# Order of the weight splits and choice of the weight homes in a two-layer decoder trunk

## Chip, cores and metric

One NeuronCore of one Trainium2 chip runs the whole kernel; the other cores are idle. The metric is the device time of one execution in microseconds (us), the median over several executions. PE is the matrix engine (PEld its weight loads), DVE the vector engine, ACT the scalar engine, POOL the general engine that here only issues accumulating transfers, SP the engine that issues the plain transfers.

## What is computed

Two decoder layers on an input of 512 tokens by 1024 features, all in fp32. Each layer is a gated FFN, a mixer and a second gated FFN:

```python
def swiglu(h, w_gate, w_up, w_down):
    return (jax.nn.silu(h @ w_gate) * (h @ w_up)) @ w_down

for l in range(DEPTH):            # 2 layers, D_MODEL 1024, D_FF 2816, SEQ 512
    h = rms_norm(x, gn[0])
    x = x + 0.5 * rms_norm(swiglu(h, ffn1...), gn[1])
    proj = rms_norm(x, gn[2]) @ w_in[l]
    ...
    mixed = jax.nn.sigmoid(gate_a) * y_hg + jax.nn.sigmoid(gate_b) * y_at
    x = x + rms_norm(mixed @ w_out[l], gn[3])
    x = x + 0.5 * rms_norm(swiglu(rms_norm(x, gn[4]), ffn2...), gn[5])
```

`y_hg` is a chunked linear recurrence over four heads, `y_at` a sliding-window attention; the change touches neither. It touches the way the weights of all these products reach PE.

## The kernel before

**Three products for one.** PE multiplies rounded fp32 operands. Every operand is therefore kept as a pair: `hi`, the value rounded by a copy into the matmul type, and `lo`, the remainder. One product is three matmuls, hi·hi, hi·lo and lo·hi (`mm3`). An activation pair is made by `split` (L432 the copy to `hi` on ACT, L433 the subtraction to `lo` on DVE). A weight pair lives in a *home*: two tiles `whi` and `wlo` of 128 x 1024, of which there are six (`WS`).

**The weight stream.** The object `ws` of class `Stream` holds a list of items in the order in which PE uses them. SP loads the raw weights (`w32` in the code, `w` in the profile; L247, 512 KB each) into four slots, in order; a load waits until the last reader of the unit that had the slot is done. `split` (a method of `Stream`, L324 to L373) turns the next item into a home. There are these kinds of items:
- `u`: ACT copies to `whi` (L354), DVE subtracts to `wlo` (L363). The first items of the kernel are of this kind.
- `v`: ACT copies to `whi`, ACT writes minus the weight into `wlo` (L358), and POOL issues a transfer that adds the weight to `wlo` on its way (L361). This takes DVE out of the work.
- `a`, `b`, `c`, `d`: two raw units u and u+1 make one group of a seven-product scheme in the gated FFNs and in the mixers' gates. `a` is unit u, made as `v` is. `b` needs a first sum of the two units (L340, L341 on DVE, into a tile `tt`), then a cast and a DVE subtraction. `c` needs the second sum (L347, L348), then the same. `d`, the half item, is half of unit u+1, 512 columns, made as `v` is; PE uses it four times, the others eight times.
- `p1` to `p7`: quarter items of the FFNs' second product, made by `quarter` (L288 cast, L296 subtraction).

PE uses a, b, c, d of one group in this order, and before the change they are split in this order too. `ahead` keeps some three items split ahead of PE, as homes are free. Before the change the six homes rotate: an item takes the home that is next in turn, and waits until PE has let go of the item that was there.

**Who orders what.** PE's order is the order of the code. The rows of the other engines are put in order by a scheduler, save where the code pins a row to its place in the program (`pin`, and `ws.hold` inside the loop `fast`, where `ws.tight` is set). Each engine then runs its rows strictly one after another: a row that waits for a semaphore holds all rows behind it.

**Stages.** In time: the start (eight column blocks of x are loaded and split, their squares are summed, L462 on ACT and L463 on DVE; `rstd` makes 1/rms, L475 on ACT, L476 and L477 on DVE, and a matmul with `ones` spreads it); then for each layer FFN 1, mixer, FFN 2. An FFN has a loop over groups (`fast`, 84 matmuls of 256 columns a group, DVE steps L1063 to L1087 between the seven products) and a stage `down` of quarter items. There are four such loops: 89 to 233 us (15 groups), 728 to 915, 1062 to 1247 and 1742 to 1928 us (19 groups each). They are called stages 1 to 4 below.

Of the kernel before, what the change touches and what calls it, by code (L numbers as in the profile page):

```python
# [8 lines left out]
F32R = mybir.dt.float32r  # L9
# [6 lines left out]
P = 128  # L16
D = 1024
# [19 lines left out]
W32, WS, AHEAD, TAIL, FIRST, EARLY, LATE = 4, 6, 3, 4, 7, 4, 8  # L37
# [9 lines left out]
def trunk(ctx: ExitStack, tc: tile.TileContext, xin, wall, gains, lbT, hgain, sinks, c_dist, c_mask, c_ident, out):  # L47
    nc = tc.nc
    cp = ctx.enter_context(tc.tile_pool(name="cp", bufs=1))
    sb = ctx.enter_context(tc.tile_pool(name="sb", bufs=1))  # L50
# [9 lines left out]
    def nm(s):  # L60
        seq[0] += 1
        return f"{s}_{seq[0]}"
# [18 lines left out]
    class Order:  # L81
        def __init__(self):
            self.t = 0.0
            self.rest = 0.0
            self.cos = []
# [62 lines left out]
    pin = tc.keep_in_program_order  # L148
# [10 lines left out]
    class Stream:  # L159
        def __init__(self):  # L160
            self.n, self.wall = 0, 0
            self.items = []
            self.raw, self.dma = {}, 0
            self.done, self.flight = 0, 0
            self.cur, self.c = 0, 0
            self.src = {}
            self.pinned = False
            self.most = AHEAD
            self.tight, self.gate = False, None
            self.side, self.freed = [], 0  # L170
            self.part = {}

        def plain(self, n, kind="u", at=0):
# [84 lines left out]
        def quarter(self, it):  # L258

            q, u, v, h = it.q, it.u, it.u + it.n, (slice(0, S), slice(S, D))  # L260

            def sums(o, x, y, op):
                for c in range(2):
                    pin(nc.vector.tensor_tensor(o[c], x[c], y[c], op=op))  # L264

            def raw(i):
                self.load(i + 1)
                return [self.raw[i][:, c] for c in h]

            def leave(i):  # L270
                self.raw.pop(i)
                self.freed += 1
                self.load(self.freed + W32)

            if it.kind in ("p1", "p2"):
                w = raw((u if it.kind == "p1" else v) + q)
            elif it.kind in ("p3", "p5"):
                w = self.b22[q]
            elif it.kind == "p7":

                w = self.b12[q]
                if q == 0:
                    sums(w, w, self.b22[q], ALU.add)
            else:
                w = self.b12[q]
            it.hi, it.lo = (sb.tile([P, D + 64], F32R, tag=t, name=nm(t), bufs=WS)[:, it.at : it.at + D] for t in ("whi", "wlo"))
            for c in range(2):
                i = nc.scalar.copy(it.hi[:, h[c]], w[c])  # L288
                if self.pinned:
                    pin(i)  # L290
            if it.kind == "p7" and q + 1 < it.n:
                sums(self.b12[q + 1], self.b12[q + 1], self.b22[q + 1], ALU.add)
            elif it.kind == "p6":
                sums(self.b22[q], self.b22[q], w, ALU.add)
            for c in range(2):
                pin(nc.vector.tensor_tensor(it.lo[:, h[c]], w[c], it.hi[:, h[c]].bitcast(F32), op=ALU.subtract))  # L296
            if it.kind == "p7":

                sums(w, raw(u + q), w, ALU.subtract)
                leave(u + q)  # L300
            elif it.kind == "p5":
                self.b22[q] = None
                if q + 1 < it.n:
                    sums(self.b12[q], raw(v + q), self.b12[q], ALU.add)
                    leave(v + q)
            elif it.kind == "p4":
                self.b12[q] = None
                if q == 0:
                    i = it.n - 1
                    sums(self.b12[i], raw(v + i), self.b12[i], ALU.add)  # L310
                    leave(v + i)
            self.done += 1
            self.flight += 1
# [5 lines left out]
        def product(self):  # L319
            if self.gate:  # L320
                self.gate()
                self.gate = None

        def split(self):  # L324
            it = self.items[self.done]
            if it.kind[0] == "p":
                return self.quarter(it)
            u, last = it.u, it.kind in "uvd"
            self.load(u + (1 if it.kind in "uv" else 2))
            it.hi, it.lo = (sb.tile([P, D + 64], F32R, tag=t, name=nm(t), bufs=WS)[:, it.at : it.at + D] for t in ("whi", "wlo"))  # L330
            w, h = self.raw[u], (slice(0, D // 2), slice(D // 2, D))
            cols = (slice(0, D),)
            if it.kind == "u" and u < 2:
                cols = h
            if it.kind in "bcd":
                v = self.raw[u + 1]
            if it.kind == "b":

                self.t13 = sb.tile([P, D], F32, tag="tt", name=nm("tt"), bufs=2)
                pin(nc.vector.tensor_tensor(self.t13[:, h[0]], w[:, h[0]], v[:, h[0]], op=ALU.add))  # L340
                pin(nc.vector.tensor_tensor(self.t13[:, h[1]], v[:, h[0]], v[:, h[1]], op=ALU.add))  # L341
                w = self.t13
                self.product()
            elif it.kind == "c":

                t = sb.tile([P, D], F32, tag="tt", name=nm("tt"), bufs=2)
                pin(nc.vector.tensor_tensor(t[:, h[0]], self.t13[:, h[0]], v[:, h[1]], op=ALU.add))  # L347
                pin(nc.vector.tensor_tensor(t[:, h[1]], t[:, h[0]], w[:, h[1]], op=ALU.add))  # L348
                w = t
            elif it.kind == "d":  # L350
                w = v
                cols = h[1:]
            for c in cols:
                i = nc.scalar.copy(it.hi[:, c], w[:, c])  # L354
                if u < 6 or self.pinned or self.tight:
                    pin(i)
                if it.kind in "vad":
                    i = nc.scalar.mul(it.lo[:, c], w[:, c], -1.0)  # L358
                    if self.pinned or self.tight:
                        pin(i)  # L360
                    nc.gpsimd.dma_start(it.lo[:, c].bitcast(F32), w[:, c], accum_op=ALU.add)  # L361
                else:
                    self.hold(nc.vector.tensor_tensor(it.lo[:, c], w[:, c], it.hi[:, c].bitcast(F32), op=ALU.subtract))  # L363
            self.done += 1
            self.flight += 1
            if last:
                nu = u + (1 if it.kind in "uv" else 2)
                for i in range(u, nu):
                    self.raw.pop(i)
                    self.freed += 1  # L370
                self.load(self.freed + W32)

        def ahead(self):  # L373
            while self.done < min(len(self.items), self.cur + 1 + self.most) and self.flight < WS:
                self.split()

        def need(self, i):
            self.ahead()
            while self.done <= i:
                assert self.flight < WS  # L380
                self.split()
            return self.items[i]
# [117 lines left out]
    def pair_split(v, how=split):  # L500
        return how(v, to=(big(F32R, [P, 2, S // 2]), big(F32R, [P, 2, S // 2])))
# [13 lines left out]
    class First(Quarters):  # L515
# [44 lines left out]
        def sums(self):  # L560

            k = len(self.x56)
            a = []
            for i in range(2):
                f = xs[k + 4 * i]
                nc.vector.scalar_tensor_tensor(f, f, g_sb[:, 0, 0, k + 4 * i : k + 4 * i + 1], self.rb, op0=ALU.mult, op1=ALU.mult)
                a.append([f[:, c] for c in HALF])
            self.x124.append([])
            for v in (a[0][0], a[1][0], a[1][1]):
                x = big(F32R, [P, 2, S // 2])  # L570
                split(v, to=(x[:, 0, :], x[:, 1, :]))
                self.x124[k].append(x)
            for x, v in zip((self.x56, self.x37), quarter_sums(a[0][0], a[1][0], a[0][1], a[1][1])):
                x.append(pair_split(v))
# [74 lines left out]
    class Late:  # L649
# [20 lines left out]
        def first(self, k):  # L670
            x = big(F32R, [P, 2, S // 2])
            self.x1.append(split(self.src[k][:, HALF[0]], to=(x[:, 0, :], x[:, 1, :]), hold=pin))
# [979 lines left out]
```

## Time and profile before

| | |
|---|---|
| median of 3 runs | 2052.01 us (2051.7 to 2052.35) |
| profiled execution, its own time | 2052.22 us |
| span of the profile | 2050.4 us |
| granted clock, mean | 0.999 |
| PE busy | 2035.9 us, 99% |
| DVE busy | 1623.6 us, 79% |
| ACT busy | 1250.1 us, 61% |
| POOL busy | 267.6 us, 13% |
| raw weights and other reads | 213.43 MB, 111 GB/s over the span |

Rows of the timeline read: start, duration, engine, line, operation, output tile and input tiles, shape; in brackets how long the engine was idle before the row, and what ended the idle time. A row `x4` is four instructions in succession, and its duration runs from the first start to the last end. A row that begins with two names and an arrow says who waited for what, how long in all, how often, and the longest time. Rows of one engine can overlap by about 0.1 us, since an instruction starts before the one ahead of it has left the pipeline.

### The profile page before, as it was taken

How to read it: one execution, taken by the hardware profiler on the slowest of the kernel's cores; microseconds unless marked ns; L12 is line 12 of the kernel's file. 1: busy time of each engine (PE TensorE's matmuls, PEld its weight loads, DVE VectorE, ACT ScalarE, POOL GpSimd, SP SyncE). 2: the span in 40 equal slices, each digit the busy share in tenths (PEclk: the TensorE clock that was granted, in tenths of full speed). 3: DMA queues.
4: the chain of work that ended last, by engine and by line, in shares of the span. 5: the costliest groups of instructions: out<-in, count | busy, mean ns of one | idle time of the engine just before them, and what ended most of it. 6: DMA issues, size and time to landing. Idle time of an engine off the chain costs nothing. (4 is left out here: it accounts for less than half of the span.)

```text
span 2050.4 us, 36557 instructions
## 1 busy us (share of the span) xinstructions
PE 2035.9 (99%) x13553; PEld 1820.7 (89%) x13553; DVE 1623.6 (79%) x2894; ACT 1250.1 (61%) x2213; POOL 267.6 (13%) x318
## 2 busy tenths in 40 slices
PE   9999999999999999999999999999999999999998
PEld 8899978877888999998899998888778989999977
DVE  5887889767676778888988878987686858788888
ACT  7566687446355556658866566864554545665684
POOL 0111140000000011113201111400000100111140
PEclk9999999999999999999999999999999999999999
DMA  8577798322237367778757878872122563777794
GB/s 257 146 189 193 184 195 238 117 64 71 73 94 215 114 147 190 189 190 205 203 154 188 193 187 205 181 229 92 62 73 62 136 194 102 181 188 190 184 201 123
DMA packets 166802, 328.07 MB, mean 160 GB/s; under 512 B 19072, under 2 KB 85088, under 8 KB 166624
## 3 DMA queue, kind: packets, MB, share of 16 engines
q1 hardware_dynamic: 122416, 228.16, 33.2%
q0 software_dynamic: 44064, 97.54, 28.2%
q8 instruction: 106, 1.74, 0.3%
q14 instruction: 72, 0.59, 0.1%
q10 hardware_dynamic: 144, 0.05, 0.0%
HBM read 213.43 MB, written 14.73 MB: 111 GB/s over the span
## 5 line engine op out<-in xcount | busy, mean ns | idle before, releaser
L116 PE MATMUL acc<-s,whi 128*128 128x256 f32 (+1 forms) x4998 | 1027.5, 305 | 0.0
L116 PEld LDWEIGHTS acc<-s,whi 128*128 128x128 f32 x4998 | 794.7, 188 | 46.5 <-issue 3.2
L116 PE MATMUL acc<-s,wlo 128*128 128x256 f32 (+1 forms) x2488 | 757.0, 304 | 3.3 <-DMA wlo<-w 2.9
L116 PEld LDWEIGHTS acc<-s,wlo 128*128 128x128 f32 x2488 | 469.1, 189 | 28.7 <-DMA wlo<-w 5.0
L116 PE MATMUL acc<-whi,s 128*128 128x512 f32 x1360 | 442.4, 393 | 2.6 <-DVE s L433 1.8
L354 ACT CAST whi<-w 128x1024 fp32r<-128x1024 f32 (+1 forms) x310 | 286.5, 928 | 148.2 <-PE acc L116 105.2
L354 ACT CAST whi<-tt 128x1024 fp32r<-128x1024 f32 x160 | 168.0, 1050 | 250.2 <-DVE tt L348 164.7
L361 POOL DMA_DIRECT2D wlo<-w x178 | 154.0, 867 | 1235.6 <-DVE wlo L363 504.8
L116 PEld LDWEIGHTS acc<-whi,s 128*128 128x128 f32 x1360 | 255.0, 188 | 61.4 <-issue 3.2
L363 DVE TENSOR_TENSOR wlo<-tt,whi 128x1024 fp32r<-128x1024 f32 x160 | 196.0, 1225 | 131.9 <-ACT whi L354 126.0
L116 PE MATMUL acc<-wlo,s 128*128 128x512 f32 x680 | 266.4, 392 | 0.9 <-DVE wlo L296 0.9
L116 PE MATMUL aux<-s,whi 128*128 128x256 f32 (+1 forms) x1296 | 230.0, 280 | 0.0
L363 DVE TENSOR_TENSOR wlo<-w,whi 128x1024 fp32r<-128x1024 f32 (+1 forms) x132 | 157.3, 1205 | 73.9 <-ACT whi L354 73.6
L116 PEld LDWEIGHTS aux<-s,whi 128*128 128x128 f32 x1296 | 197.0, 188 | 1.1 <-issue 0.5
L116 PE MATMUL aux<-s,wlo 128*128 128x256 f32 (+1 forms) x648 | 181.1, 279 | 0.0
L116 PEld LDWEIGHTS acc<-wlo,s 128*128 128x128 f32 x680 | 127.8, 188 | 29.8 <-DVE wlo L296 5.1
L358 ACT ACTIVATE wlo<-w 128x1024 fp32r<-128x1024 f32 (+1 forms) x178 | 153.7, 863 | 0.0
L116 PE MATMUL aux<-whi,s 128*128 128x512 f32 x432 | 144.1, 391 | 0.0
L444 POOL DMA_DIRECT2D s<-s x128 | 111.1, 971 | 216.1 <-ACT s L432 98.1
L116 PEld LDWEIGHTS aux<-s,wlo 128*128 128x128 f32 x648 | 122.1, 188 | 0.5 <-DMA wlo<-w 0.2
L296 DVE TENSOR_TENSOR wlo<-s,whi 128x512 fp32r<-128x512 f32 x160 | 102.7, 685 | 9.9 <-ACT whi L288 6.3
L432 ACT CAST s<-s 128x512 fp32r<-128x512 f32 (+1 forms) x140 | 70.8, 547 | 44.8 <-DVE s L491 39.3
(184 smaller groups left out, 2468.7 us busy)
## 6 DMA issues: line engine op xcount, KB each, us to landing
w<-wall SPq DMA_DIRECT2D x267, 512.0 KB, 4.2
wlo<-w POOLq DMA_DIRECT2D x98, 512.0 KB, 5.2
w<-wall SPq DMA_DIRECT2D x224, 128.0 KB, 3.5
wlo<-w POOLq DMA_DIRECT2D x80, 256.0 KB, 3.3
s<-wall SPq DMA_DIRECT2D x128, 128.0 KB, 4.4
s<-s POOLq DMA_DIRECT2D x64, 256.0 KB, 4.9
x_d<-s SPq DMA_DIRECT2D x48, 256.0 KB, 4.1
s<-x_d SPq DMA_DIRECT2D x48, 256.0 KB, 5.1
```

The source lines that it names most:

```text
L116: nc.tensor.matmul(o, lhsT, rhs, start=start, stop=stop)
L296: pin(nc.vector.tensor_tensor(it.lo[:, h[c]], w[c], it.hi[:, h[c]].bitcast(F32), op=ALU.subtract))
L354: i = nc.scalar.copy(it.hi[:, c], w[:, c])
L358: i = nc.scalar.mul(it.lo[:, c], w[:, c], -1.0)
L361: nc.gpsimd.dma_start(it.lo[:, c].bitcast(F32), w[:, c], accum_op=ALU.add)
L363: self.hold(nc.vector.tensor_tensor(it.lo[:, c], w[:, c], it.hi[:, c].bitcast(F32), op=ALU.subtract))
L432: (hold or ws.hold)(nc.scalar.copy(hi, src))
L444: nc.gpsimd.dma_start(lo.bitcast(F32), src, accum_op=ALU.add)
```

## The change

Three things change in the class `Stream`.
1. **Order of the splits.** A table `plan` puts d ahead of c of the same group: a, b, d, c. Where there is a home left after d, c is split in the same call.
2. **Order inside an item** of the kinds v, a, d: the copy with a minus sign and its transfer come ahead of the cast to `whi`.
3. **Homes.** Each of the six homes is a tile of its own name (`whi0` to `whi5`), and `home` picks the one whose last item was used up longest ago, in place of the rotation.

The raw units are let go after c now, no longer after d, and `need` asks if the item has its home. The diff:

```diff
         self.side, self.freed = [], 0
+            self.own, self.plan = [None] * WS, []
...
-            it.hi, it.lo = (sb.tile([P, D + 64], F32R, tag=t, name=nm(t), bufs=WS)[:, it.at : it.at + D] for t in ("whi", "wlo"))
+            self.home(it)
...
+        def home(self, it):
+
+            k = min((k for k in range(WS) if not self.own[k] or self.own[k].left <= 0), key=lambda k: self.own[k].i if self.own[k] else -1)
+            self.own[k] = it
+            it.hi, it.lo = (sb.tile([P, D + 64], F32R, tag=f"{t}{k}", name=nm(t))[:, it.at : it.at + D] for t in ("whi", "wlo"))
+
         def split(self):
-            it = self.items[self.done]
+            if not self.plan:
+                for i, it in enumerate(self.items):
+                    it.i = i
+                    self.plan.append(i)
+                    if it.kind == "d":
+                        self.plan[-2:] = [i, i - 1]
+            it = self.items[self.plan[self.done]]
...
             for c in cols:
-                i = nc.scalar.copy(it.hi[:, c], w[:, c])
-                if u < 6 or self.pinned or self.tight:
-                    pin(i)
                 if it.kind in "vad":
                     i = nc.scalar.mul(it.lo[:, c], w[:, c], -1.0)
                     if self.pinned or self.tight:
                         pin(i)
                     nc.gpsimd.dma_start(it.lo[:, c].bitcast(F32), w[:, c], accum_op=ALU.add)
-                else:
+                i = nc.scalar.copy(it.hi[:, c], w[:, c])
+                if u < 6 or self.pinned or self.tight:
+                    pin(i)
+                if it.kind not in "vad":
                     self.hold(nc.vector.tensor_tensor(it.lo[:, c], w[:, c], it.hi[:, c].bitcast(F32), op=ALU.subtract))
             self.done += 1
             self.flight += 1
-            if last:
+            if it.kind in "uvc":
...
+            elif it.kind == "d" and self.flight < WS:
+                self.split()
...
-            while self.done <= i:
+            while not hasattr(self.items[i], "hi"):
```

The diff shifts later lines by 14 (L354 becomes L372, L358 becomes L368, L363 becomes L376, L432 becomes L446, L462 becomes L476). PE's order is the same row by row, and so is POOL's; SP's differs in three places by one load that moves ahead of two stores; DVE's differs at the kernel's start and around the mixers' gates. ACT's differs throughout. Three places of it follow; in the names, the number behind `whi`, `wlo`, `s` counts the tiles, and `w_33_174` is the raw unit in a slot.

First ACT at the start of the kernel, with the last four squares of x (`s_203` to `s_212`) and the first weights. Before:

```order
L532 ACTIVATE s_199<-s_77,g_sb 128x512
L462 ACTIVATE s_203<-s_74 128x512
L462 ACTIVATE s_206<-s_75 128x512
L462 ACTIVATE s_209<-s_76 128x512
L462 ACTIVATE s_212<-s_77 128x512
L354 CAST whi_248<-w_18_142 128x1024
L354 CAST whi_278<-w_23_154 128x1024
L354 CAST whi_308<-w_33_174 128x1024
```

and now:

```order
L546 ACTIVATE s_199<-s_77,g_sb 128x512
L372 CAST whi_308<-w_33_174 128x1024
L476 ACTIVATE s_203<-s_74 128x512
L476 ACTIVATE s_206<-s_75 128x512
L476 ACTIVATE s_209<-s_76 128x512
L476 ACTIVATE s_212<-s_77 128x512
L372 CAST whi_248<-w_18_142 128x1024
L372 CAST whi_278<-w_23_154 128x1024
```

The cast of `w_33` moved from behind the four squares and the casts of `w_18` and `w_23` to a place ahead of them all. On DVE its subtraction (`wlo_309`) moved in the same way: it stands ahead of the sums of squares with `s_203`, `s_206` and `s_209` now, and the last sum, with `s_212`, stands behind the subtraction of `w_18` (`wlo_249`).

Second ACT at the start of stage 2, where the last activations of the norm ahead are split (`s` <- `s`, L432). Before:

```order
L1106 ACTIVATE s_7905<-acc_7609 128x512
L432 CAST s_7919<-s_7913 128x512
L432 CAST s_7923<-s_7914 128x512
L354 CAST whi_7928<-tt_7930 128x1024
L354 CAST whi_7935<-w_1389_7568 128x512
L358 ACTIVATE wlo_7936<-w_1389_7568 128x512
L354 CAST whi_7968<-w_1405_7640 128x1024
L358 ACTIVATE wlo_7969<-w_1405_7640 128x1024
L432 CAST s_7983<-s_7977 128x512
```

and now:

```order
L1120 ACTIVATE s_7905<-acc_7609 128x512
L372 CAST whi_7968<-w_1405_7640 128x1024
L446 CAST s_7919<-s_7913 128x512
L368 ACTIVATE wlo_7969<-w_1405_7640 128x1024
L446 CAST s_7923<-s_7914 128x512
L372 CAST whi_7933<-tt_7935 128x1024
L446 CAST s_7983<-s_7977 128x512
```

The cast and the copy of the next group's a (from `w_1405`) moved from behind c's cast to places ahead of and between the casts of the activations; d's pair (from `w_1389`) moved further up still, out of this piece. Stages 3 and 4 begin in the same way; in stage 1 the cast of the second group's a (from `w_135`) stands ahead of the last two casts of activations, and its copy between them.

Third ACT inside a loop, one group of stage 2. Before:

```order
L354 CAST whi_8189<-tt_8191 128x1024
L354 CAST whi_8220<-w_1453_7942 128x512
L358 ACTIVATE wlo_8221<-w_1453_7942 128x512
L354 CAST whi_8256<-w_1481_8098 128x1024
L358 ACTIVATE wlo_8257<-w_1481_8098 128x1024
L1084 ACTIVATE m_8238<-m_8238 128x512
L354 CAST whi_8283<-tt_8285 128x1024
```

and now:

```order
L368 ACTIVATE wlo_8190<-w_1453_7942 128x512
L372 CAST whi_8189<-w_1453_7942 128x512
L372 CAST whi_8218<-tt_8220 128x1024
L368 ACTIVATE wlo_8257<-w_1481_8098 128x1024
L372 CAST whi_8256<-w_1481_8098 128x1024
L1098 ACTIVATE m_8238<-m_8238 128x512
L372 CAST whi_8283<-tt_8285 128x1024
```

d's pair (from `w_1453`) moved ahead of c's cast (from a `tt`), and in d and the next a the copy moved ahead of the cast.

More of the change, by code (lines that the diff above doesn't have):

```diff
@@ L322, in product @@
                 self.gate = None
+        def home(self, it):
+            k = min((k for k in range(WS) if not self.own[k] or self.own[k].left <= 0), key=lambda k: self.own[k].i if self.own[k] else -1)
+            self.own[k] = it
+            it.hi, it.lo = (sb.tile([P, D + 64], F32R, tag=f"{t}{k}", name=nm(t))[:, it.at : it.at + D] for t in ("whi", "wlo"))
         def split(self):
-            it = self.items[self.done]
+            if not self.plan:
[5 more added lines that the diff above has]
+            it = self.items[self.plan[self.done]]
             if it.kind[0] == "p":
                 return self.quarter(it)
-            u, last = it.u, it.kind in "uvd"
+            u = it.u
             self.load(u + (1 if it.kind in "uv" else 2))
-            it.hi, it.lo = (sb.tile([P, D + 64], F32R, tag=t, name=nm(t), bufs=WS)[:, it.at : it.at + D] for t in ("whi", "wlo"))
-            w, h = self.raw[u], (slice(0, D // 2), slice(D // 2, D))
+            self.home(it)
+            w, h = self.raw.get(u), (slice(0, D // 2), slice(D // 2, D))
             cols = (slice(0, D),)
@@ L365, in split @@
             self.flight += 1
-            if last:
-                nu = u + (1 if it.kind in "uv" else 2)
-                for i in range(u, nu):
+            if it.kind in "uvc":
+                for i in range(u, u + (2 if it.kind == "c" else 1)):
                     self.raw.pop(i)
```

## The prediction

> **What bounds the kernel now.** I read the waits of PE's weight loads first, then single rows of the timeline in the loops, then the rows of ACT and DVE at every place where the new order of ACT differs. PE is busy for nearly the whole span, so a change can only win what PE still waits, and lose where it makes PE wait. The waits over all of the run and in stages 2 and 3 alone:
>
> ```profile
> PEld acc L116 <- DMA wlo<-w: 5.0, 9, 1.8
> ...
> PEld acc L116 <- DMA wlo<-w: 0.6, 2, 0.3
> ...
> PEld acc L116 <- DMA wlo<-w: 2.8, 4, 1.8
> ...
> PEld acc L116 <- ACT whi L288: 1.3, 1, 1.3
> PEld acc L116 <- DVE s L433: 1.1, 1, 1.1
> ```
>
> The first row is the whole kernel: nine waits, 5.0 us, for the accumulating transfer into `wlo`, which POOL issues after ACT's copy. The second and third are the loops of stages 2 and 3. The last two stand in `down` of stage 3. The transfer waits are what an earlier d and an earlier copy attack. But what sets the end of a stage is another thing:
>
> ```profile
> 724.71 0.68 DVE L347 TENSOR_TENSOR tt<-tt,w 128x512 f32<-128x512 f32 x1
> 917.35 0.68 DVE L296 TENSOR_TENSOR wlo<-w,whi 128x512 fp32r<-128x512 f32 x1
> 1058.84 0.68 DVE L347 TENSOR_TENSOR tt<-tt,w 128x512 f32<-128x512 f32 x1
> 1251.79 0.68 DVE L296 TENSOR_TENSOR wlo<-w,whi 128x512 fp32r<-128x512 f32 x1
> 1738.21 0.68 DVE L347 TENSOR_TENSOR tt<-tt,w 128x512 f32<-128x512 f32 x1
> 1930.83 0.68 DVE L296 TENSOR_TENSOR wlo<-w,whi 128x512 fp32r<-128x512 f32 x1
> L354 ACT CAST whi<-tt 128x1024 fp32r<-128x1024 f32 x160 | 168.0, 1050 | 250.2 <-DVE tt L348 164.7
> ```
>
> From the first second sum (L347) of a stage to its first quarter item (L296), stage 2 takes DVE 192.64 us, stage 3 192.95, stage 4 192.62, though PE waits 0.6 us in the one loop and 2.8 in the next. DVE and ACT hand sums and casts to each other at a pace of their own, and PE, when it is early, waits in `down` (the rows L288 and L433 above). So a PE that is earlier in a loop only waits longer behind it. The last row says where the moved d fits: ACT is idle 164.7 us in all before c's casts, waiting for L348, about 2.5 us a group over the 64 groups that have it. The pace stays.
>
> **Start: the largest term.** The profile's rows on ACT, DVE, SP's queue and PE:
>
> ```profile
> 19.39 2.18 ACT L462 ACTIVATE s<-s 128x512 f32<-128x512 f32 x4
> 21.47 2.12 ACT L354 CAST whi<-w 128x1024 fp32r<-128x1024 f32 x2
> 25.25 1.05 ACT L354 CAST whi<-w 128x1024 fp32r<-128x1024 f32 x1 [1.66 <-DMA w<-wall]
> ...
> 29.01 1.05 ACT L354 CAST whi<-w 128x1024 fp32r<-128x1024 f32 x1 [1.45 <-DMA w<-wall]
> ...
> 31.21 1.05 ACT L354 CAST whi<-w 128x1024 fp32r<-128x1024 f32 x1 [0.20 <-DMA w<-wall]
> 32.17 1.05 ACT L358 ACTIVATE wlo<-w 128x1024 fp32r<-128x1024 f32 x1
> 33.24 1.28 ACT L475 ACT_TABLE_LOAD   x1
> 34.53 0.26 ACT L475 ACTIVATE rc<-aux,eps_t 128x4 f32<-128x4 f32 x1
> ...
> 24.21 4.62 DVE L363 TENSOR_TENSOR wlo<-w,whi 128x1024 fp32r<-128x1024 f32 x4
> 35.04 0.69 DVE L477 TENSOR_TENSOR s<-ident,rc 128x512 f32<-128x512 f32 x1
> ...
> 25.46 0.33 SPq L247 DMA_DIRECT2D w<-wall  x1
> 26.60 0.33 SPq L247 DMA_DIRECT2D w<-wall  x1
> ...
> 28.51 0.62 PE L116 MATMUL acc<-s,whi 128*128 128x512 f32 x2
> 28.96 0.39 PE L116 MATMUL acc<-s,wlo 128*128 128x512 f32 x1
> 36.26 1.02 PE L116 MATMUL aux<-s,ones 128*128 128x512 f32 x2
> ```
>
> The cast at 25.25 is that of `w_33`; its raw unit lands just then. It now stands ahead of the four squares (19.39) and the casts of `w_18` and `w_23` (21.47), so ACT stands still from about 19.5 to 25.25 and these six rows wait behind it. Step by step: `w_33` from 25.25; the squares from 26.25, 2.08 for four; the cast of `w_18` from 28.3 to 29.4. PE wants that home at 28.51 and its `wlo` at 28.96; DVE's subtraction (4.62 for four, so 1.22 alone) ends at 30.6. PE is 1.7 us late here.
>
> Then the delay feeds itself. The load of `w_56` waits for that subtraction to free its slot: it left at 25.46 and leaves at 30.65. In the profile its cast began 3.55 us after (29.01), now at 34.2; its copy, 0.95 behind, at 35.15. The load of `w_59` leaves behind the subtraction of `w_23`, which has one more sum of squares ahead of it, at about 32.4. Before, 26.60 to 31.21, that was 4.61 us under more load; with 3.55 ACT is still busy until 36.1, with 4.61 the cast begins at 37.0. I take 36.4, nearer the first, as fewer transfers run beside it. Copy 37.4 (0.96), table load 38.4 (1.07, from 32.17 to 33.24), square root 39.7 (1.29), L477 40.2 (0.51) to 40.9. PE wants L477's result at 36.26: **4.7 us** late, the 1.7 being part of it (ends 4.4 and 5.3). Nothing hides this: the waiting matmul holds all of PE, and the norm (so DVE's and ACT's later work) hangs on it.
>
> A sentence aside: the Trainium skill, page "DMA: Bandwidth & Descriptors", section "Anatomy of one DMA", gives about 2.0 us plus bytes over 436 GB/s, an estimate of 3.2 us for 512 KB; by it the two loads come 0.35 us sooner and the term would be near 4.3, and the trace's 3.55 is above it.
>
> **Starts of the stages.** Stage 1, then stage 2 for the three alike:
>
> ```profile
> 82.48 0.61 PE L116 MATMUL acc<-s,whi 128*128 128x512 f32 x2
> 83.49 1.15 ACT L432 CAST s<-s 128x512 fp32r<-128x512 f32 x2 [2.03 <-DVE s L491]
> 90.77 1.03 ACT L354 CAST whi<-tt 128x1024 fp32r<-128x1024 f32 x1
> ...
> 721.93 0.61 PE L116 MATMUL acc<-s,whi 128*128 128x512 f32 x2
> 722.85 1.14 ACT L432 CAST s<-s 128x512 fp32r<-128x512 f32 x2 [3.20 <-DVE s L491]
> 726.63 1.05 ACT L354 CAST whi<-tt 128x1024 fp32r<-128x1024 f32 x1 [2.65 <-DVE tt L348]
> 729.05 0.42 DVE L491 SCALAR_TENSOR_TENSOR s<-s,s 128x256 f32<-128x256 f32 x1
> 730.54 1.12 ACT L432 CAST s<-s 128x512 fp32r<-128x512 f32 x2
> ```
>
> The cast of the next a waits for a home that PE lets go at 722.55 (the end of the row 721.93) and then goes first: 722.6. The first cast of activations starts at 723.6 in place of 722.85, the copy follows, the second starts at 725.05 in place of 723.37 (half-way in the x2). DVE's split of it, both second sums and c's cast follow 1.6 later (726.63 to 728.2), and so does L491. The casts at 730.54 stood behind d and a and do so no more; they wait for L491 alone and come at 731.1. The chain that sets the stage is 0.57 later, three times: **1.7** (ends 0 and 3 x 1.6 = 4.8, if nothing is made good). Stage 1 in the same manner: home free at 83.09, second cast 1.5 late, of which b's cast at 90.77, no longer behind four rows, makes good 0.4: **1.1** (0 to 1.5).
>
> **Mixers.**
>
> ```profile
> 602.42 0.19 PEld L116 LDWEIGHTS acc<-s,wlo 128*128 128x128 f32 x1 [0.67 <-DMA wlo<-w]
> ...
> 589.37 1.23 DVE L363 TENSOR_TENSOR wlo<-tt,whi 128x1024 fp32r<-128x1024 f32 x1 [1.48 <-ACT whi L354]
> ...
> 592.13 0.28 PE L116 MATMUL acc<-s,wlo 128*128 128x256 f32 x1
> ```
>
> The wait at 602.42 is behind a copy that moves up: **-0.7**. Against it, ahead of c's cast there now stand a cast and a copy of a plain item that wait for PE. By my replay c's remainder, ready at 590.60 now, comes 1.3 to 1.6 later; PE wants it at 592.13. I put 0.1 in each mixer, **0.2** (0 to 1.6).
>
> **Loops.** Of the other 4.3 us of transfer waits nothing is left after `down`, by the first part: **0**. The ends are -8.5 (below) and 0. The new waits for homes (c takes b's, 24 matmuls later) lie behind ACT's own order by over 2 us; c's cast waits for L348 anyway. The moved copies take their transfers along: POOL issues those of d and a in the same order, only sooner, and SP's next load, which waits for both readers of a raw unit, is held by c's sums and not by d's transfer any more. Both only add slack. If the room before L348 were not there, d's cast and copy, each by estimate half of a 1.05 us row of twice the columns, would lengthen each group by 1.1 us; the 2.5 us a group say that the room is there.
>
> Sum: 4.7 + 1.1 + 1.7 + 0.2 - 0.7 = **+7.0**. On the profiled execution's 2052.22 that is 2059.2; the median of the runs lies 0.2 below, so 2059.0.
>
> **Rivals.**
> *The loops keep their gain.* If PE, not the ACT and DVE chain, set the stages, the 4.3 us of waits would be won, and PE's pace too, which differs by stretch:
>
> ```profile
> 800.00:900.00 100.00, 100.00 (x852) 100.00 (x851) 81.53 (x116) 61.12 (x83) 18.08 (x21) 1.00 0.79 189
> 1130.00:1220.00 90.00, 90.00 (x793) 89.81 (x792) 71.93 (x101) 55.38 (x75) 15.51 (x18) 1.00 0.79 192
> ```
>
> 852 matmuls in 100 us are 117.4 ns each, 793 in 90 are 113.5; the slow pace lasts some 130 us in stage 2, 4.2 us of loss. With both, -8.5: 2050.5, not slower. The equal DVE times speak against it. Chance 0.10. It decides if L347 to L296 gets shorter than 192.6.
> *The start is hidden.* If the scheduler's row of `w_33` found its unit in SBUF early, or rms were not on PE's path, only 7.0 - 4.7 = 2.3 is left: 2054.3. The 1.66 us wait before that very row speaks against it. 0.13.
> *The slow pace spreads.* The pace changes at small stalls, and the new order makes one at each stage's start. A whole loop of 19 x 84 matmuls at 3.9 ns more is 6.2 us; stage 3 could hide some 2.4 of it (the two `down` waits). One such stage more: +4, 2063. 0.12.
> *PE's clock.* PE stands still some 3.0 us (from 38.0 to 40.9). Were its clock to fall to half for as long afterwards, it would lose some 1.7: 2060.7. No row shows a granted clock under 1.00. The Trainium skill, page "TensorE: Matmul & The Clock Gate", section "Part 1: The HAM clock gate", says that after an idle window of 3.4 us the clock halves; 3.0 falls just short. 0.08.
> My forecast has the other 0.57.
>
> **How the numbers follow.** Predicted 2059.0. The terms' bounds alone give 2055 to 2063; the range 2053 to 2064 takes in the hidden start, the spread pace and the clock, and leaves out the loops' gain. What this kernel's runs can tell from no change is about 0.2%, 4.1 us, so slower means above 2056.1: nearly all of my forecast and the last two rivals, 0.75. Within it: the hidden start, half of the loops' gain and the low tail, 0.17. Faster 0.08.
>
> **What would show it.** Right: on ACT the cast of `w_33` at 25.2 directly behind L546 with about 5 us idle; PE's matmul with `ones` near 41; L360 to L297 (before, L347 to L296) still about 192 us with the waits for `wlo` in the loops gone and those in `down` longer; the casts L446 at the stages' starts on both sides of a copy. Wrong: `ones` near 36, or stages that are shorter on DVE.

## The result and the profile after

The changed kernel takes 2059.65 us (median of 7 runs, 2059.28 to 2060.87); the kernel before takes 2052.47 us in the same comparison. The ratio is 1.0035, with an interval of 1.0025 to 1.0045: slower by 7.2 us, clear of the 0.2% that can be told. The forecast was 2059.0, 7.0 over the median of the kernel before. The profiled execution of the changed kernel is the slowest of its seven, 2060.87 us, with a span of 2059.1.

The start, in the timeline of the changed kernel (ACT, SP's queue, DVE, PE):

```profile
18.86 0.71 ACT L546 ACTIVATE s<-s,g_sb 128x512 fp32r<-128x512 f32 x1
25.48 1.05 ACT L372 CAST whi<-w 128x1024 fp32r<-128x1024 f32 x1 [5.91 <-DMA w<-wall]
26.43 2.19 ACT L476 ACTIVATE s<-s 128x512 f32<-128x512 f32 x4
28.52 3.94 ACT L372 CAST whi<-w 128x1024 fp32r<-128x1024 f32 x4
...
34.78 1.04 ACT L372 CAST whi<-w 128x1024 fp32r<-128x1024 f32 x1 [1.35 <-DMA w<-wall]
...
36.80 1.28 ACT L489 ACT_TABLE_LOAD   x1
38.10 0.26 ACT L489 ACTIVATE rc<-aux,eps_t 128x4 f32<-128x4 f32 x1
...
26.56 1.23 DVE L376 TENSOR_TENSOR wlo<-w,whi 128x1024 fp32r<-128x1024 f32 x1 [5.17 <-ACT whi L372]
...
27.81 3.66 SPq L248 DMA_DIRECT2D w<-wall  x2
...
29.61 0.73 PE L116 MATMUL acc<-s,whi 128*128 128x512 f32 x2 [1.32 <-ACT whi L372]
31.17 0.51 PE L116 MATMUL acc<-s,wlo 128*128 128x512 f32 x1 [0.83 <-DVE wlo L376]
39.44 1.10 PE L116 MATMUL aux<-s,ones 128*128 128x512 f32 x2 [0.67 <-DVE s L491]
```

ACT stands still for 5.91 us in front of the cast of `w_33`, as forecast, and the squares (26.43) and the casts of `w_18` and `w_23` (the first two of the four at 28.52) come behind it. PE waits three times, and its matmul with `ones` comes at 39.44 where it came at 36.26: 3.2 us, where 4.7 were forecast. The start of stage 2:

```profile
727.86 1.05 ACT L372 CAST whi<-w 128x1024 fp32r<-128x1024 f32 x1 [2.99 <-issue]
728.82 0.62 ACT L446 CAST s<-s 128x512 fp32r<-128x512 f32 x1
729.34 1.05 ACT L368 ACTIVATE wlo<-w 128x1024 fp32r<-128x1024 f32 x1
730.30 0.60 ACT L446 CAST s<-s 128x512 fp32r<-128x512 f32 x1
733.46 1.05 ACT L372 CAST whi<-tt 128x1024 fp32r<-128x1024 f32 x1 [2.57 <-DVE tt L361]
736.33 1.14 ACT L446 CAST s<-s 128x512 fp32r<-128x512 f32 x2 [1.82 <-DVE s L505]
...
731.54 0.69 DVE L360 TENSOR_TENSOR tt<-tt,w 128x512 f32<-128x512 f32 x1
738.20 0.68 DVE L353 TENSOR_TENSOR tt<-w,w 128x512 f32<-128x512 f32 x1
923.43 0.68 DVE L297 TENSOR_TENSOR wlo<-w,whi 128x512 fp32r<-128x512 f32 x1
```

PE reaches this place 5.23 us later than before, from the start, stage 1 and the mixer. Of the casts of activations, the first comes 5.97 later (728.82 for 722.85), c's cast 6.83 (733.46 for 726.63), and the next casts 5.79 (736.33 for 730.54): 1.6 of lateness, of which all but 0.56 is made good, as the replay had it. From L360 to L297 DVE takes 191.9 us, 0.75 less than before, since 1.0 is made good behind L360 and 0.3 is lost on the way: in the loop a group takes DVE 9.73 us where it took 9.71 (L1063, now L1077, from one group to the next). The waits of PE's weight loads over the whole run, in the kernel before (two rows) and after the change (three):

```profile
PEld acc L116 <- DVE wlo L296: 5.1, 12, 0.7
PEld acc L116 <- DVE s L433: 3.2, 4, 1.1
...
PEld acc L116 <- DVE wlo L297: 6.7, 16, 1.2
PEld acc L116 <- DVE s L447: 5.1, 7, 1.1
PEld acc L116 <- DMA wlo<-w: 2.5, 6, 0.7
```

The waits for the accumulating transfers are half of what they were (5.0). The waits for DVE's L297, all of them in `down`, are 1.6 us longer. Of the 5.1 us for L447, three times 0.5 stand at the starts of stages 2, 3 and 4, where the late split now holds PE itself, and the rest is in `down` as before. What the loops win, `down` takes back.

### The profile page after: what moved, and what is told of

The parts are those of the page before. It is cut to its first block, busy times and chain, and to the rows that moved or that the text cites. A ratio compares the mean times of both kernels' runs of the same rounds, so it can differ in the third digit from the quotient of the medians.

```text
span 2059.1 us, 36336 instructions
## 1 busy us (share of the span) xinstructions
PE 2043.0 (99%) x13553; PEld 1826.4 (89%) x13553; DVE 1623.9 (79%) x2894; ACT 1250.3 (61%) x2213; POOL 267.5 (13%) x318
## 4 chain that ended last, share of the span: by engine, by line
PE 38%; issue 7%; DVE 4%; DMA 2%; ACT 1%; POOL 1%; SPq 0%; POOLq 0%; DVEq 0%; ACTq 0%
PE acc L116 29%; PE aux L116 8%; DVE wlo L297 1%; DMA wlo<-w 1%; DMA w<-wall 1%; PE aux L126 1%; POOL wlo L371 1%; DVE wlo L376 1%; DVE s L447 0%; DMA s<-wall 0%; DVE s L265 0%; PE acc L126 0%; ACT whi L372 0%; ACT whi L289 0%; SPq L245 0%
## 5 line engine op out<-in xcount | busy, mean ns | idle before, releaser
L372 ACT CAST whi<-w 128x1024 fp32r<-128x1024 f32 (+1 forms) x310 | 286.1, 927 | 195.5 <-PE acc L116 120.4
L376 DVE TENSOR_TENSOR wlo<-tt,whi 128x1024 fp32r<-128x1024 f32 x160 | 196.0, 1225 | 127.1 <-ACT whi L372 125.9
L372 ACT CAST whi<-tt 128x1024 fp32r<-128x1024 f32 x160 | 167.9, 1049 | 153.5 <-DVE tt L361 95.4
L376 DVE TENSOR_TENSOR wlo<-w,whi 128x1024 fp32r<-128x1024 f32 (+1 forms) x132 | 157.6, 1206 | 77.7 <-ACT whi L372 77.1
L368 ACT ACTIVATE wlo<-w 128x1024 fp32r<-128x1024 f32 (+1 forms) x178 | 154.3, 867 | 0.5 <-PE aux L116 0.5
L1098 ACT ACTIVATE m<-m 128x512 f32<-128x512 f32 x72 | 45.6, 634 | 151.5 <-DVE m L1084 151.5
L297 DVE TENSOR_TENSOR wlo<-s,whi 128x512 fp32r<-128x512 f32 x160 | 102.7, 685 | 9.9 <-ACT whi L289 8.1
```

The source lines that it names most:

```text
L1098: ws.hold(nc.scalar.activation(out=m[:, 0:2, :], in_=m[:, 0:2, :], func=AF.Silu))
```

## Experiments

Each kernel ran beside the kernel before on the same chip, in three groups: 1 to 4, 5 to 7 (on another chip than the rest) and 8 to 10, in which the kernel before took 2052.61, 2052.29 and 2052.75 us. The table gives, from the profiles, how much later than in the kernel before the same matmul of PE starts, at six places (us; PE's order is the same in all of them). It shows where each kernel loses or wins. Each row is a single execution: that of the change is the slowest of its seven, that of the order only the slowest of its eleven (2050.22), that with the start pinned the fastest of its eleven (2056.09).

| kernel | behind the start (41) | end of stage 1 (300) | start of stage 2 (716) | end of stage 2 (990) | end of stage 3 (1345) | near the end (2040) | median |
|---|---|---|---|---|---|---|---|
| the change | 3.3 | 4.6 | 5.2 | 6.1 | 7.1 | 8.6 | 2059.65 |
| start pinned | 0.2 | 1.4 | 1.2 | 2.1 | 2.9 | 3.9 | 2056.7 |
| homes only | 3.8 | 4.6 | 4.6 | 5.4 | 6.0 | 7.1 | 2058.88 |
| copy first only | 0.2 | -0.1 | -1.0 | -0.9 | -0.7 | -0.2 | 2052.07 |
| order and copy, no homes | -0.2 | -0.2 | -1.2 | -1.8 | -1.8 | -2.1 | 2050.17 |
| order only | 0.3 | 0.0 | -0.6 | -1.3 | -1.8 | -2.0 | 2048.87 |
| longer chain | 0.0 | 1.4 | 0.4 | 1.3 | 2.3 | 3.4 | 2055.62 |
| c's remainder later | 0.2 | -4.2 | -4.6 | -11.6 | -18.6 | -25.7 | 2025.85 |
| the change, c later | 4.1 | -0.3 | -1.3 | -7.2 | -13.7 | -20.8 | 2032.85 |
| order only, c later | -0.2 | -4.6 | -5.8 | -12.8 | -19.4 | -26.3 | 2028.5 |
| before, c later | 0.0 | -4.5 | -5.7 | -12.3 | -19.3 | -20.0 | 2036.47 |

**1. The start pinned.** The changed kernel, with the cast of the seventh unit (`w_33`) kept in its place:

```diff
-                if u < 6 or self.pinned or self.tight:
+                if u < 7 or self.pinned or self.tight:
                     pin(i)
```

> The changed kernel with one more of the first casts pinned, so that the cast of w_33 stands behind the four squares again. Theory (the start costs what the profile shows there, 3.2 us, and all that follows is only moved): PE's matmul with ones back near 36.3, and the time 3.2 us under the changed kernel, about 2056.4. Rival (the lateness of the start is made good later where PE waits anyway, so its removal gives nothing): 2059 to 2060.

2056.7 us (11 runs), ratio 1.002 (1.0011 to 1.0029), 3.0 us under the changed kernel's 2059.65. PE's matmul with `ones` is at 36.37. The start is worth what the profile showed there, and nothing later makes it good. What is left, 4.1 us by the medians, lies at the stages.

**2. Named homes alone,** the kernel before with two edits:

```diff
+            self.own = [None] * WS
...
-            it.hi, it.lo = (sb.tile([P, D + 64], F32R, tag=t, name=nm(t), bufs=WS)...)
+            self.home(it)
...
         def split(self):
             it = self.items[self.done]
+            it.i = self.done
```

> The kernel before with only the six named homes; the splits in the order a, b, c, d, casts ahead of copies. Theory (named homes alone let the scheduler move the early casts up, at the start and at the four stage starts): PE's ones near 39.4, all of the loss, 2058 to 2061, and the waits for wlo in the loops as in the kernel before. Rival (d ahead of c does it): 2051.5 to 2053.

2058.88 us (6 runs), ratio 1.003 (1.0019 to 1.0042). Timeline of PE and ACT in this kernel:

```profile
25.36 1.05 ACT L362 CAST whi<-w 128x1024 fp32r<-128x1024 f32 x1 [5.99 <-DMA w<-wall]
...
29.49 0.73 PE L116 MATMUL acc<-s,whi 128*128 128x512 f32 x2 [1.23 <-ACT whi L362]
31.06 0.50 PE L116 MATMUL acc<-s,wlo 128*128 128x512 f32 x1 [0.83 <-DVE wlo L371]
40.05 1.02 PE L116 MATMUL aux<-s,ones 128*128 128x512 f32 x2
```

The same 6 us of ACT and the same first two waits of PE. The third is not there: the matmul with `ones`, at 40.05 (39.4 was expected), waits for nothing, since PE itself ran at half its clock for 3.41 us from 31.61 and came late (see PE's clock, below). ACT's rows show the same early casts at the starts of stages 2 to 4 as in the changed kernel. The named homes alone bring 6.3 us of loss by the medians, and the change 7.2, with intervals that overlap: nearly all of the loss is the homes'. With them, d first and the copy first win nothing, though without them they win 2.4 us (experiment 4).

**3. The copy first alone:**

```diff
             for c in cols:
-                i = nc.scalar.copy(it.hi[:, c], w[:, c])
-                if u < 6 or self.pinned or self.tight:
-                    pin(i)
                 if it.kind in "vad":
                     ...
-                else:
+                i = nc.scalar.copy(it.hi[:, c], w[:, c])
+                if u < 6 or self.pinned or self.tight:
+                    pin(i)
+                if it.kind not in "vad":
```

> The kernel before with only the copy and its transfer ahead of the cast in v, a, d. Theory (DVE and ACT set the stages): waits for wlo in the loops fall by half or more, L347 to L296 stays at 192.6, the time 2051 to 2053. Rival (loop waits are worth their size): 2 to 4 us less, 2048 to 2050.

2052.07 us (11 runs), ratio 0.9998 (0.9989 to 1.0007): no change that can be told. A miss in one point: the waits for `wlo` did not fall (6.5 us in its profile, 5.0 before). The time is as the theory had it.

**4. Order and copy, without the homes.** The changed kernel with the line `self.home(it)` put back to the rotating tiles in both places.

> The changed kernel with the rotation of the six homes in place of the named homes: d ahead of c and the copy first stay. Theory: start and stage starts as before, the waits for wlo gone from the loops, PE waits longer in down, the mixer's wait gone: 2051 to 2052.5. Rival (the loops keep their gain): 2044 to 2048. A third: d now takes the home that c's group let go late and waits for it in the loops, 2054 or more.

2050.17 us (11 runs), ratio 0.9988 (0.998 to 0.9997): a little faster than before. Here too the waits for `wlo` stay (4.9 us). That is under the expected 2051 to 2052.5: the 2.4 us are over three times the 0.7 of the mixer that were counted. The table puts most of the rest in stage 2, and a little in stage 4.

**5. The order alone:** the kernel before with the table `plan` and no other part of the change.

> The kernel before with d split ahead of c, rotating homes, casts ahead of copies. Theory (the stages are set by DVE and ACT): 2050 to 2052.5, L360 to L297 (before L347 to L296) still 192.6 us. Rival (d ahead of c wins the wlo waits of the loops): 2046 to 2049. If the copy first is what makes the 2.4 us of the run with both, this stays at 2052.

2048.87 us (11 runs), ratio 0.9985 (0.9976 to 0.9993). That is below the theory's range and just inside the rival's, so the time alone speaks for the rival. The order of the splits is what wins the 2.4 us of experiment 4; the copy first adds nothing to it. The ACT rows at the start of stage 2 show another source than the loops:

```profile
726.05 1.05 ACT L367 CAST whi<-tt 128x1024 fp32r<-128x1024 f32 x1 [2.70 <-DVE tt L361]
727.01 1.04 ACT L367 CAST whi<-w 128x1024 fp32r<-128x1024 f32 x1
727.95 1.06 ACT L371 ACTIVATE wlo<-w 128x1024 fp32r<-128x1024 f32 x1
728.91 1.12 ACT L446 CAST s<-s 128x512 fp32r<-128x512 f32 x2
```

d's two rows, which stood between the casts of c and the next a before, are gone from here, done earlier. The casts of the activations start 2.86 us behind c's cast in place of 3.91 (726.63 to 730.54 before), so the chain of DVE and ACT enters the stage a microsecond sooner; by the table PE wins 0.5 to 0.7 of it in stages 2 and 3 and less in stage 4. From L360 to L297 DVE takes 191.9, 192.2 and 191.9 us in stages 2, 3 and 4, some 0.75 less than before in each, while the pace inside the loop is no shorter than before. So the gain is made at the stage's start, not in the loop, as far as this profile, 1.35 us over the median, can tell.

**6. A longer chain,** to test what sets the stages:

```diff
         ws.hold(nc.vector.tensor_tensor(v, pairs[1], m[:, 2:3, :].to_broadcast([P, 2, H2]), op=ALU.add))
+        if ws.tight:
+            pin(nc.vector.tensor_copy(s, s))
```

> The run with rotating homes, d first and copy first, and in each of the 72 loop groups one more DVE row, a copy of 256 columns of a tile that nobody reads any more, between the steps that combine the products; the output stays the same. It lengthens the pace of DVE and ACT by 0.2 to 0.34 us a group and touches neither PE nor a transfer. Theory (DVE and ACT set the stages): 14 to 25 us longer, 2064 to 2075. Rival (PE sets the loops, DVE has room): at most 4 us longer, 2050 to 2054.

2055.62 us (10 runs), ratio 1.0015 (1.0006 to 1.0025): 5.4 us over the run without the row (experiment 4). The theory expected 14 to 25 and the rival at most 4, so the time by itself does not decide. DVE's rows of one group of this kernel, and of one group without the row:

```profile
759.35 0.68 DVE L1077 TENSOR_TENSOR m<-acc,s 128x512 f32<-128x512 f32 x1
760.07 0.69 DVE L1079 TENSOR_TENSOR s<-acc,m 128x512 f32<-128x512 f32 x1
760.68 0.28 DVE L1081 COPY s<-s 128x256 f32<-128x256 f32 x1
760.88 0.42 DVE L1085 TENSOR_TENSOR m<-acc,s 128x256 f32<-128x256 f32 x1
...
769.15 0.69 DVE L1077 TENSOR_TENSOR m<-acc,s 128x512 f32<-128x512 f32 x1
```

```profile
757.65 0.68 DVE L1077 TENSOR_TENSOR m<-acc,s 128x512 f32<-128x512 f32 x1
...
767.38 0.68 DVE L1077 TENSOR_TENSOR m<-acc,s 128x512 f32<-128x512 f32 x1
```

The pace goes from 9.73 to 9.80 us a group, 0.07, since the copy fills a part of the time in which the next row waited for the row before it anyway (0.73 from start to start there before, 0.61 and 0.20 now). 72 groups by 0.07 are 5.0, and 5.4 were measured; from L360 to L297 DVE takes 1.1, 1.4, 1.1 and 1.4 us longer in the four stages. What the chain loses a group comes out at the end in full. The theory held, the price of the row did not.

**7. c's remainder later.** In a group DVE waits 1.2 us for ACT's cast of c. Its subtraction is put behind the first combination of the products (L1063 of the kernel before), so that this row fills the wait. On top of experiment 4:

```diff
-                if it.kind not in "vad":
-                    self.hold(nc.vector.tensor_tensor(it.lo[:, c], w[:, c], ...))
+                if it.kind not in "vad":
+                    def rest(it=it, c=c, w=w):
+                        self.hold(nc.vector.tensor_tensor(it.lo[:, c], w[:, c], ...))
+                    if it.kind == "c" and self.tight and self.between:
+                        it.late = self.late = rest
+                    else:
+                        rest()
...
         ws.hold(nc.vector.tensor_tensor(m[:, 0:4:2, :], pairs[0], ...))
+        ws.flush()          # emits self.late
+        ws.between = False  # set to True at the start of the group
```

> The run with rotating homes, d first and copy first, with c's remainder on DVE placed behind the first combination of the products (L1063 of the kernel before), so that DVE works while ACT casts c, where it is idle 1.17 us a group now. Theory (DVE and ACT set the stages at 9.70 us a group, PE needs 9.53 at its fast pace): the pace falls to about 9.1, PE sets the loops, 4 to 12 us less: 2038 to 2046; the waits of PE for L297 and L447 in down get shorter. Rival (PE sets the loops already): 2049 to 2051. A third: the combination now waits for PE's product 6 and gives the gap back, 2048 to 2050.

2025.85 us (4 runs, 2025.0 to 2030.91), ratio 0.9877 (0.9862 to 0.9892): 26 us under the kernel before, and twice the most that was expected. DVE's rows, and the waits of PE's weight loads over the whole run:

```profile
768.80 0.69 DVE L1091 TENSOR_TENSOR m<-acc,s 128x512 f32<-128x512 f32 x1 [0.39 <-PE acc L116]
769.61 1.23 DVE L378 TENSOR_TENSOR wlo<-tt,whi 128x1024 fp32r<-128x1024 f32 x1
...
778.32 0.69 DVE L1091 TENSOR_TENSOR m<-acc,s 128x512 f32<-128x512 f32 x1 [0.90 <-PE acc L116]
```

```profile
PEld acc L116 <- DVE wlo L298: 2.1, 5, 0.7
PEld aux L116 <- DVE eps_t L139: 1.1, 1, 1.1
```

From the fifth group of a stage on, at the latest, DVE waits for PE in the groups, and the pace is PE's, 9.52 us here. The estimate had counted the loops alone (72 groups by 0.2 at most). `down` gained as well: DVE and ACT are there in time, the waits for L297 and L447 fall from 4.9, 2.5 and 4.1 us (experiment 4) to 2.1, and those for `wlo` from 4.9 to 0.5. The third point is PE's pace, below.

**8, 9, 10. The same edit on the changed kernel, with the order alone, and on the kernel before.**

> The changed kernel, named homes and all, with c's remainder behind the first combination. It separates the two ways in which the named homes cost time: the start, 3.2 us, is a wait of PE itself, while the late casts at the stage starts cost only through the chain of DVE and ACT. Theory: with that chain off the limit, only the start stays, and about 0.5 us of direct waits of PE at the three later stage starts: 3 to 5 us above the run of rotating homes with the same edit (2025.9), so 2029 to 2031. Rival (the stage starts cost PE directly): 7 to 9 us above it, 2033 to 2035.

> Rotating homes, d ahead of c, casts ahead of copies, c's remainder behind the first combination. Theory: the order of copy and cast matters only for the transfer's landing; with PE as the limit of the loops some waits for wlo may come back: 2025 to 2028. Rival (copy first is worth nothing at all): the same as with it, 2025.5 to 2026.2.

> The kernel before with nothing but c's remainder behind the first combination. Theory: when PE sets the loops the waits for wlo, 5.0 us in the kernel before, count in full or grow, since d and a are still split late: 2028 to 2034. Rival (the order of d and the copy does not matter here either): 2025 to 2027.

Four runs each. On the changed kernel: 2032.85 us (2031.39 to 2043.93), ratio 0.9913 (0.9887 to 0.994). Its profile stands 3.9 us behind that of experiment 7 after the start and 4.8 behind near the end; the profiled executions are 2031.39 and 2026.53. Of the 3.9, some 0.8 comes with the half clock, which PE had here too from 31.72 on. So without the chain as a limit the start stays, and the stage starts cost PE about 1 us. The medians are 7.0 apart, but the runs of one kernel scatter by 6 us and more (below), so the rest is not settled by them. With the order alone: 2028.5 (2025.11, 2025.94, 2031.05, 2031.88), ratio 0.9885 (0.9867 to 0.9902); whether the copy first is worth anything there was not decided. On the kernel before: 2036.47 (2032.2 to 2044.07), ratio 0.9923 (0.9897 to 0.9949), above the expected span. Its profile, of the fastest of its four runs, has 0.5 us of waits for `wlo` in all, where the kernel before has 5.0, so the reason given in the expectation was wrong. What it shows is PE's pace, by windows of 100 us in stages 2, 3 and 4:

```profile
760.00:860.00 100.00, 100.00 (x885) 100.00 (x884) 82.83 (x118) 65.73 (x88) 18.96 (x22) 1.00 0.83 197
1100.00:1200.00 100.00, 100.00 (x884) 100.00 (x884) 82.05 (x116) 63.09 (x84) 18.14 (x21) 1.00 0.84 197
1760.00:1860.00 100.00, 100.00 (x851) 100.00 (x850) 79.53 (x113) 63.07 (x84) 18.10 (x21) 1.00 0.79 191
```

885 matmuls in 100 us are 113.0 ns each, 851 are 117.5. In stage 4 this execution kept the slow pace. In that loop (1742 to 1928 us of the kernel before) it lost 1.1 us against the kernel before, where experiment 7 won 5.4: 6.5 us for one loop.

## Why the prediction was right, step by step

- **What bounds the kernel.** Right, and shown from both sides: a longer chain costs its length (experiment 6), a shorter one gives PE its own pace (7). That the chain sets the stages, and so takes back what the loops win, was read from three equal times of DVE across stages with different waits of PE.
- **The start.** The path was right, from the late cast over the squares and the loads to the matmul with `ones`; the size was not: 4.7 was forecast, 3.2 came. The step that failed is "The load of `w_56` waits for that subtraction to free its slot: it left at 25.46 and leaves at 30.65." In the changed kernel `w_33` is subtracted ahead of `w_18`, so its slot is the first to come free, at 27.8, and the load leaves then (SP's row above). The load of `w_59`, on which the rest hangs, then leaves behind the subtraction of `w_18`, at 31.14, and not behind that of `w_23`, at 32.4. It took 3.54 us (31.14 to 34.68), where the sum used 4.0, and the load of `w_56` took 3.50 (27.81 to 31.31); both are above the aside's 3.2. The fit behind those 3.2 us (the Trainium skill, page "DMA: Bandwidth & Descriptors", section "Anatomy of one DMA") is headed there for the gpsimd path, and these loads are SP's. Of the three waits of PE, the last is therefore short. Pinning that one cast gave 3.0 us back (experiment 1).
- **Stage starts.** 1.1 and three times 0.57 were forecast. Stage 1 costs 1.3 in the table (3.3 to 4.6), and 1.2 in the run with the pinned start. Stage 2: DVE enters the loop 0.58 later than PE's own lateness (5.81 and 5.23), as forecast; 0.3 more goes in the loop and 0.3 in `down`. By the table stages 2, 3 and 4 lose about 0.9, 1.0 and 1.5 with the short pieces ahead of them (mixer 2 included), 3.4 in all, and 2.7 in the run with the pinned start; 1.8 was forecast for all of this. The named homes are the cause (experiment 2 has the loss, 4 has not). That they act by the scheduler's early casts is read from ACT's rows, which have them in 2 and not in 4; no run pinned these casts. This term was too small by 0.9 to 1.6 us, that of the start too large by 1.5.
- **Mixers.** -0.7 and +0.2 were forecast. In the profile PE loses 0.3 at c's remainder in each mixer, where 0.1 was put, and wins 0.7 at the wait for the copy in the first.
- **Loops: 0.** Right in sum. That the waits for `wlo` vanish was wrong: in stage 2 they are 1.0 us after the change, 0.6 before, and in the whole run 2.5. The sign that was to decide, a time from L347 to L296 under 192.6, came in part (191.9 in stage 2), though the chain did not get faster: the lateness made good behind L360 shortens that time, and the pace of the groups, 9.71 before and 9.73 after, is the better sign.
- **Rivals.** The loops' gain did not stay, and the start was not hidden. The slow pace did spread. Stage 3 of the changed kernel and of the kernel before:

```profile
1140.00:1240.00 100.00, 100.00 (x852) 100.00 (x851) 81.02 (x115) 60.02 (x81) 18.09 (x21) 1.00 0.79 186
```

```profile
1130.00:1230.00 100.00, 99.89 (x878) 99.50 (x877) 80.08 (x112) 61.64 (x84) 17.23 (x20) 1.00 0.79 191
```

852 for 878 matmuls in 100 us. PE was 8.8 us behind at the end of this loop and 7.3 after the first rows of `down`: most of the slow pace was taken out of waits that were there anyway. It was priced as 4 us and cost little, because the chain, not PE, ended the stage. In experiment 10 it is not hidden any more.
- **PE's clock.** In the profile of the changed kernel it did not fall at the start, but that was luck. The clock goes by stretches of 3.41 us (last section). Two of them in this kernel, and two in experiment 2 (length, PE's busy time, and in the third place from the end the granted clock):

```profile
26.81:30.22 3.41, 2.09 (x9) 1.20 (x7) 3.20 (x5) 3.41 (x6) 0.00 (x0) 1.00 0.38 109
30.22:33.63 3.41, 2.58 (x12) 2.04 (x12) 3.41 (x4) 3.21 (x4) 0.00 (x0) 1.00 0.53 174
```

```profile
28.19:31.61 3.42, 1.35 (x5) 0.78 (x5) 3.21 (x6) 3.42 (x5) 0.00 (x0) 1.00 0.43 153
31.61:35.02 3.41, 3.41 (x9) 2.64 (x8) 2.27 (x2) 2.00 (x3) 1.00 (x1) 0.50 0.74 219
```

  The first two waits of PE are nearly the same in both, 1.32 and 0.83 us, 1.23 and 0.83. In experiment 2 they fell into one stretch, and the clock was halved for the next; in the changed kernel they fell into two. The idle window of 3.4 us that the prediction quotes from the Trainium skill (page "TensorE: Matmul & The Clock Gate", section "Part 1: The HAM clock gate") agrees with these stretches in its length, but PE was busy for 1.35 us of the one behind which the clock fell; the measurement decides. The half clock made PE some 1.5 us later, but 1.0 of that came out of the third wait: the matmuls at 41 us are 3.8 late in place of 3.3. The prediction's 1.7 was too much for its own words too, since half a clock for 3.0 us costs 1.5. And one row does show a clock under 1.00: the mean of 0.999 before the change is the half clock of the last 3 us, behind PE's last matmul.
- **The size of the profile.** The profiled execution is 8.65 us over that of the kernel before, the medians differ by 7.2. About 1.0 of it is lost at 320 us, in stage 1's `down`, where ACT's casts of quarter items had waited for their raw weights at 288 and 292 us; the same place costs 0.1 in the run with the pinned start and 0.4 in experiment 2, so most of it seems to belong to that execution. That the sum of 7.0 met the median so closely is in part luck, two errors of opposite sign. The range was drawn a little narrow: the ends of the terms without the loops add up to +3.7 and +12.5, or 2055.7 to 2064.5, where the prediction says 2055 to 2063.

## What to carry to other kernels

Look at what every engine's queue has behind a row that moved: one cast that waits 6 us for its load cost 3 us of the matrix engine here, by the squares and casts behind it. When two engines hand work to each other at a pace of their own, and that pace is longer than the third engine's, the third engine's waits are worth nothing; here only the shorter chain of experiment 7 made them count. The time from one row to the same row of the next group shows the pace. And freeing a buffer earlier can change the scheduler's order: compare the order of the rows, at the start above all, before the gain is counted.

## What the runs showed of the hardware

A stream of equal matmuls of 256 columns has two paces, 113.0 and 117.5 ns from start to start, at a granted clock of 1.00 in both. A loop keeps one for tens of microseconds up to its whole length. It changes at short waits of PE (0.7 us at 1858 in the kernel before, 0.1 us at 1741.8 in experiment 10), though not at each (1.1 us at 1828 in experiment 3 changed nothing). Where PE is the limit, one loop of 19 groups at the slow pace cost 6.5 us (experiment 10). The runs of experiment 9 fall into two pairs, 2025.1 and 2025.9, 2031.1 and 2031.9, which one slow loop would explain; only a fast one was profiled. What chooses the pace was not found.

The granted clock goes by stretches of 3.413 us. In the clock records of all twelve profiles it changes only at whole multiples of that time from the record's first entry: at 8 in experiments 2 and 8, 74 in 3, 75 in 6, and 601 in the changed kernel, at its end. It fell to half behind each such stretch in which PE's rows, whose ends are modelled, cover 0.52 of the time or less: 0.40 and 0.34 at the start in experiments 2 and 8, 0.49 and 0.45 in `down` of stage 1 in 3 and 6, 0.52 at the end of the kernel before. It did not fall behind any of the other stretches, some 7100; the least busy of them are at 0.54 (the kernel before, at 1119) and 0.57 (experiment 3, at 1914). So waits of 1.2 and 0.8 us were enough when they fell into one stretch.
